# Attention in blocks of queries: the products with the values are issued one step later

## The chip, the cores and the metric

The kernel runs on one core of a Trainium2 chip. The metric is the device time of one execution in microseconds (us), as a median of repeated runs. The core has a matrix engine (PE, whose weight loader PEld loads the stationary operand of each matmul), a vector engine (DVE), a scalar engine (ACT), GpSimd (POOL), and the sync engine (SP), which issues most transfers. Each engine works through its own instructions in the order in which they stand; semaphores make one wait for another.

## The reference, cut to what matters

One layer of a decoder: a recurrent branch and an attention branch are merged, then comes a mixture of experts. The change touches the attention branch only: 8 heads, 1024 tokens, causal, in blocks of 128 queries.

```python
    for s0 in range(0, S, Q_BLOCK):                  # Q_BLOCK = 128, S = 1024
        e = s0 + Q_BLOCK
        s = jnp.einsum("bqhd,bkhd->bhqk", q[:, s0:e], k[:, :e]).astype(jnp.float32) * scale
        mask = jnp.arange(e)[None, :] <= (s0 + jnp.arange(Q_BLOCK))[:, None]
        p = jax.nn.softmax(jnp.where(mask, s, -jnp.inf), axis=-1).astype(v.dtype)
        outs.append(jnp.einsum("bhqk,bkhd->bqhd", p, v[:, :e]))
    o = jnp.concatenate(outs, axis=1).reshape(B, S, N_HEADS * V_DIM)
    return o @ w_mla_o
```

Query block `qb` has `(qb + 1) * 128` keys, so block 7 has 1024 and block 0 has 128.

## The kernel before, in words

The program is one long straight line of stages: the input projections and the recurrent branch; the products of the recurrent branch; the attention (from about 591 us to 893 us of the span); the product with `w_mla_o` and the merge (to about 987 us); the product with `w_out` with the routing (to about 1102 us); then the experts, two to a tile of 128 rows, whose weights stream in from HBM.

Products in nearly full precision are made of three matmuls each: every operand is split into a high part (rounded by ACT, `hi_of`, L113) and a low part (the rest, by a subtraction on DVE or POOL, `lo_of`, L116), and `mm3` (L118 to L121) adds high by high, high by low and low by high.

The attention works on 64 pairs (head, block of queries), in each head in the order 6, 7, 4, 5, 2, 3, 0, 1. Each pair goes through two functions, and each two blocks through a third:

- `attn_a` (L679): the scores on PE (L693; five matmuls for up to 512 keys, ten beyond), into one of two score buffers `s` in PSUM; on DVE the mask and the row's minimum (L697); on ACT the exponential (L702); on DVE the reciprocal of the sum and the scaling (L704, L705) to the probabilities `P`.
- `attn_b` (L708): PE transposes `P` in pieces of 128 (L720) into a PSUM bank `tp`, ACT writes the high part `pth` and DVE the low part `ptl`. Two blocks of queries fill one such pair of tiles side by side; there are two buffers of each (`PT = 2`).
- `attn_c` (L724): after the second block of a pair, the products with the values: three matmuls for each block of keys (L119 `pth` by `vh`, L120 `ptl` by `vh`, L121 `pth` by `vl`), 6, 12, 18 or 24 in all, into another bank `tp`; ACT copies it out (`ot`, L735) and SP sends it to DRAM (L736).

The loop at L826 issues, at step n, `attn_a` of pair n, `attn_b` of pair n - 2 (`LA = 2`), and `attn_c` if that pair was the second of two. Between the steps it issues background work of the next heads: the products for queries, keys and values of the next two heads (`tokens_block`, L582), their norms (`tokens_end`, L606; its chain of small operations on DVE is `rsqrt`, L92 to L108), the rotation on POOL (`head_chain`), and the transposes of queries and keys (`head_T`, L646: `ks`, `qs`, `kp`, `qp`, four matmuls each, evicted by ACT and then DVE). All of these, and `attn_b` and `attn_c`, share four PSUM banks named `tp`.

The order in which these functions are called is not the order in which the instructions stand. A scheduler of the framework places the instructions of each engine when the program is built, by the order of the calls as a priority and by its own estimates of when operands and buffers are free.

Of the kernel before, what the change touches and what calls it, by code (L numbers as in the profile page):

```python
# [51 lines left out]
def block_kernel(ctx, tc, x, positions, norm1_g, w_in, conv_w, conv_b, lru_wa, lru_ba, lru_wx,  # L52
# [65 lines left out]
    def mm3(ps, lh, ll, rh, rl, start, stop):  # L118
        nc.tensor.matmul(ps, lh, rh, start=start, stop=False)  # L119
        nc.tensor.matmul(ps, lh, rl, start=False, stop=False)  # L120
        nc.tensor.matmul(ps, ll, rh, start=False, stop=stop)  # L121
# [437 lines left out]
    with pool_of(name="hd", bufs=2) as hd, \  # L559
# [119 lines left out]
        def attn_a(h, qb):  # L679
            pr, j = pairs[h // 2], h % 2  # L680
            t, rr_ = pr["t", j], pr["rr"]
            e = (qb + 1) * 128
            qsl = slice(qb * 128, e)
            ps = sps.tile([128, S], F32, name="s")
            w = e if e <= 512 else e // 2
            nw = e // w
            psv = ps.rearrange("p (a b) -> p a b", b=512)[:, 0:nw, 0:w]
            for ch in range(nw):
                cc = slice(ch * w, ch * w + w)
                for n, (a, b, r) in enumerate((("qnh", "knh", 128), ("qnh", "knl", 128),  # L690
                                               ("qnl", "knh", 128), ("qpe", "kph", 128),
                                               ("qpe", "kpl", 128))):
                    nc.tensor.matmul(psv[:, ch], t[a][0:r, qsl], t[b][0:r, cc],  # L693
                                     start=n == 0, stop=n == 4)

            nm_ = tiny.tile([128, 1], F32, name="nm_")
            nc.vector.tensor_tensor_reduce(  # L697
                psv, psv, mask[:, S - e:S].rearrange("p (a b) -> p a b", b=w),
                rr_[:, qb, j:j + 1], 3.0e38, ALU.add, ALU.min, nm_)
            P = pp.tile([128, S], F32, name="P")  # L700
            sm = tiny.tile([128, 1], F32, name="sm")
            nc.scalar.activation(P[:, 0:e].rearrange("p (a b) -> p a b", b=w), psv, AF.Exp, bias=nm_, scale=-1.0,  # L702
                                 accum_out=sm)
            nc.vector.reciprocal(sm, sm)  # L704
            nc.vector.tensor_scalar(P[:, 0:e], P[:, 0:e], sm, None, op0=ALU.mult)  # L705
            Ps[h, qb] = P

        def attn_b(h, qb):  # L708
            P = Ps.pop((h, qb))
            o0 = (qb % 2) * 128  # L710
            for w in range(qb // 4 + 1):
                if (h, qb // 2, w) not in quads:
                    quads[h, qb // 2, w] = (pp.tile([128, 4, 256], F32R, name="pth", bufs=PT),
                                            pp.tile([128, 4, 256], F32R, name="ptl", bufs=PT))
                ph_, pl_ = quads[h, qb // 2, w]
                n = min(4, qb + 1 - 4 * w)
                pt = tps.tile([128, 4, 128], F32, name="tp")
                for kb in range(n):
                    k_ = (4 * w + kb) * 128
                    nc.tensor.transpose(pt[:, kb], P[:, k_:k_ + 128], ident)  # L720
                hi_of(ph_[:, 0:n, o0:o0 + 128], pt[:, 0:n])
                lo_of(pl_[:, 0:n, o0:o0 + 128], pt[:, 0:n], ph_[:, 0:n, o0:o0 + 128], nc.vector)

        def attn_c(h, g):  # L724
            pr, j = pairs[h // 2], h % 2
            vh, vl = pr["vh"][j], pr["vl"][j]
            po = mps.tile([128, 256], F32, name="tp")
            last = 2 * g + 1
            for kb in range(last + 1):
                o0 = 128 if kb == last else 0  # L730
                ph_, pl_ = quads[h, g, kb // 4]
                mm3(po[:, o0:256], vh[:, kb], vl[:, kb], ph_[:, kb % 4, o0:256],
                    pl_[:, kb % 4, o0:256], kb == 0, kb == last)
            ot = pp.tile([128, 256], F32, name="ot", bufs=2)
            nc.scalar.activation(ot, po, AF.Copy)  # L735
            nc.sync.dma_start(o_d[h, :, g * 256:g * 256 + 256], ot)  # L736
# [84 lines left out]
        LA = 2  # L821
        QO = [6,7,4,5,2,3,0,1]
        WT = [1]*8
        seq = [(h, qb) for h in range(H) for qb in QO]
        bg, total, done, mdone = [], 0.0, 0.0, 0.0
        for n in range(len(seq) + LA):  # L826
            if n < len(seq):
                h, qb = seq[n]
                if qb == QO[0]:
                    for c, f, a in bg:  # L830
                        f(*a)
                    bg = bg_work(h)
                    total = max(1e-9, sum(c for c, f, a in bg))
                    done = mdone = 0.0
                attn_a(h, qb)
                mdone += WT[QO.index(qb)] / sum(WT) * 1.05
            if n >= LA:
                h2, qb2 = seq[n - LA]
                attn_b(h2, qb2)
                if QO.index(qb2) % 2:  # L840
                    attn_c(h2, qb2 // 2)
            if n < len(seq):
                while bg and done / total <= mdone:
                    c, f, a = bg[0]
                    if f.__name__ == "tokens_start" and QO.index(qb) < LA:
                        break
                    bg.pop(0)
                    f(*a)
                    done += c
# [745 lines left out]
```

## Time and profile before

| | |
|---|---|
| median of 3 runs | 1661.24 us (1660.24 to 1663.36) |
| the profiled execution | 1662.71 us, its span 1660.9 us, mean granted clock 0.964 |
| PE busy over the span | 91% |
| attention | 591 to 893 us |
| merge and `w_out` | 893 to 1102 us |
| experts | 1102 us to the end |

How to read the rows: a row of busy time by stretch gives, for each engine, the microseconds in which it was busy and how many instructions it ran, then the granted clock of PE as a share of full speed, the busy share of the DMA engines and GB/s. A row of waits gives who waited, for what, the total in us, how many times, and the longest. A row of the timeline gives the start, the duration, the engine, the line, the operation with output and inputs, and in brackets how long the engine sat idle before it and what ended that. PE's matmuls overlap in the records, so the pace is read from one start to the next.

### The profile page before, as it was taken

How to read it: one execution, taken by the hardware profiler on the slowest of the kernel's cores; microseconds unless marked ns; L12 is line 12 of the kernel's file. 1: busy time of each engine (PE TensorE's matmuls, PEld its weight loads, DVE VectorE, ACT ScalarE, POOL GpSimd, SP SyncE). 2: the span in 40 equal slices, each digit the busy share in tenths (PEclk: the TensorE clock that was granted, in tenths of full speed). 3: DMA queues.
4: the chain of work that ended last, by engine and by line, in shares of the span. 5: the costliest groups of instructions: out<-in, count | busy, mean ns of one | idle time of the engine just before them, and what ended most of it. 6: DMA issues, size and time to landing. Idle time of an engine off the chain costs nothing. (4 is left out here: it accounts for less than half of the span.)

```text
span 1660.9 us, 22272 instructions
## 1 busy us (share of the span) xinstructions
PE 1508.6 (91%) x8484; PEld 1141.0 (69%) x8484; DVE 723.9 (44%) x1859; ACT 499.1 (30%) x1088; POOL 470.6 (28%) x467
## 2 busy tenths in 40 slices
PE   5999999899999999999898999978998887888876
PEld 5988887788888888888787877865554453444443
DVE  7745556420001677787874446773321221221211
ACT  5324554641111366666664112210000000000000
POOL 3134443322221335252621431122221111211111
PEclk9999999899999999999999999998998997999989
DMA  6212221262345210101215655369999999999994
GB/s 193 58 47 65 58 75 55 69 224 88 102 143 171 89 39 14 36 14 36 76 33 171 221 191 197 134 244 392 364 416 418 418 419 417 414 400 411 416 405 162
DMA packets 129664, 327.71 MB, mean 197 GB/s; under 512 B 17367, under 2 KB 82337, under 8 KB 105108
## 3 DMA queue, kind: packets, MB, share of 16 engines
q1 hardware_dynamic: 111684, 295.57, 47.6%
q0 software_dynamic: 14848, 21.46, 3.6%
q10 hardware_dynamic: 3024, 9.24, 1.4%
q8 instruction: 68, 1.11, 0.3%
q14 instruction: 40, 0.33, 0.1%
HBM read 307.74 MB, written 48.59 MB: 215 GB/s over the span
## 5 line engine op out<-in xcount | busy, mean ns | idle before, releaser
L1339 PE MATMUL ph<-w,x 128*64 128x256 f32 x1104 | 163.1, 405 | 26.3 <-DMA w<-in_exp_w_dram 24.0
L116 POOL TENSOR_TENSOR w_lo<-w_raw,w_hi 128x1024 fp32r<-128x1024 f32 x40 | 98.8, 2470 | 266.3 <-ACT w_hi L113 265.7
L259 PE MATMUL pp<-uTh,w_hi 128*128 128x512 f32 x496 | 156.2, 396 | 1.1 <-ACT xp L368 1.1
L262 PE MATMUL pp<-uTl,w_hi 128*128 128x512 f32 x496 | 155.9, 395 | 0.0
L265 PE MATMUL pp<-uTh,w_lo 128*128 128x512 f32 x496 | 155.7, 395 | 0.0
L1339 PEld LDWEIGHTS ph<-w,x 128*64 128x64 f32 x1104 | 94.7, 145 | 84.3 <-DMA w<-in_exp_w_dram 26.2
L1329 DVE SCALAR_TENSOR_TENSOR hs<-ph,rec_all,hs 128x256 f32<-128x256 f32 x32 | 15.4, 482 | 289.0 <-ACT hs L1328 289.0
L1356 ACT ACTIVATE hT<-pt 128x256 f32<-128x256 f32 x32 | 12.3, 384 | 343.0 <-PE pt L1354 343.0
L259 PEld LDWEIGHTS pp<-uTh,w_hi 128*128 128x128 f32 x496 | 93.5, 189 | 23.2 <-ACT xp L368 1.1
L262 PEld LDWEIGHTS pp<-uTl,w_hi 128*128 128x128 f32 x496 | 93.6, 189 | 22.3
L265 PEld LDWEIGHTS pp<-uTh,w_lo 128*128 128x128 f32 x496 | 93.3, 188 | 22.2
L1038 PE MATMUL px<-wo,ms 128*128 128x512 f32 x384 | 97.0, 401 | 1.0 <-DVE ms L116 1.0
L1339 PE MATMUL ph<-c,x 128*64 128x256 f32 x512 | 81.3, 413 | 13.0 <-DMA c<-in_exp_w_dram 12.9
L113 ACT ACTIVATE w_hi<-w_raw 128x1024 fp32r<-128x1024 f32 x40 | 42.1, 1053 | 139.2 <-PE pp L262 110.2
L1038 PEld LDWEIGHTS px<-wo,ms 128*128 128x128 f32 x384 | 70.2, 189 | 17.5 <-issue 1.8
L1339 PE MATMUL ph<-m,x 128*64 128x256 f32 x432 | 68.0, 414 | 14.0 <-DMA m<-in_exp_w_dram 10.9
L1339 PEld LDWEIGHTS ph<-c,x 128*64 128x64 f32 x512 | 47.5, 149 | 44.2 <-DMA c<-in_exp_w_dram 15.2
L116 DVE TENSOR_TENSOR cTl<-gt,cTh 128x1024 fp32r<-128x1024 f32 x4 | 4.9, 1225 | 164.5 <-ACT cTh L113 164.5
L1368 PE MATMUL py<-w,hT 128*64 128x512 f32 x288 | 71.1, 611 | 0.5 <-ACT hT L1356 0.5
L1339 PEld LDWEIGHTS ph<-m,x 128*64 128x64 f32 x432 | 39.0, 149 | 36.1 <-DMA m<-in_exp_w_dram 9.3
L897 PE MATMUL pp<-c,w 128*128 128x512 f32 x240 | 56.9, 392 | 0.0
L120 PE MATMUL tp<-ptl,vh 128*128 128x256 f32 (+1 forms) x160 | 47.8, 299 | 9.7 <-DVE ptl L116 9.3
(657 smaller groups left out, 3379.3 us busy)
## 6 DMA issues: line engine op xcount, KB each, us to landing
w<-in_exp_w_dram SPq DMA_DIRECT2D x101, 1024.0 KB, 22.4
c<-in_exp_w_dram SPq DMA_DIRECT2D x50, 1024.0 KB, 23.3
m<-in_exp_w_dram SPq DMA_DIRECT2D x40, 1024.0 KB, 22.4
w_raw<-in_w_in_dram SPq DMA_DIRECT2D x32, 512.0 KB, 5.0
xt<-in_x_dram SPq DMA_DIRECT2D x8, 512.0 KB, 5.3
hg_d<-hh SPq DMA_DIRECT2D x8, 512.0 KB, 2.6
gt<-hg_d SPq DMA_DIRECT2D x8, 512.0 KB
sgb_d<-gt SPq DMA_DIRECT2D x8, 512.0 KB, 5.2
```

What stands on the lines that cost most here:

```text
L113: nc.scalar.activation(dst, src, AF.Copy)
L116: eng.tensor_tensor(dst, src, f32v(hi), op=ALU.subtract)
L120: nc.tensor.matmul(ps, lh, rl, start=False, stop=False)
L259: nc.tensor.matmul(ps[:, s_], wh[:, k], ah[:, k, s_], start=k == 0, stop=False)
L262: nc.tensor.matmul(ps[:, s_], wh[:, k], al[:, k, s_], start=False, stop=False)
L265: nc.tensor.matmul(ps[:, s_], wl[:, k], ah[:, k, s_], start=False, stop=k == KD - 1)
L897: nc.tensor.matmul(pb[:, s_], w[:, a, k], oT[k][b][:, s_], start=k == 0 and a + b == 0, stop=k == KD - 1 and a == 1)
L1038: nc.tensor.matmul(px[:, s_], ms[:, a, k], wos[k][:, b, s_], start=k == 0 and a + b == 0, stop=k == KD - 1 and a == 1)
L1329: nc.vector.scalar_tensor_tensor(hs, ph[:, 256:512], rst, hs, op0=ALU.mult, op1=ALU.mult)
L1339: pe(nc.tensor.matmul(ph[64 * j:64 * j + 64, wi * 256:wi * 256 + 256], xT[:, k, 64 * j:64 * j + 64], w[2 * wi + j][:, k * 256:k * 256 + 25 ...
L1356: nc.scalar.activation(hT, pt, AF.Copy)
L1368: pe(nc.tensor.matmul(py[64 * j:64 * j + 64], hT[:, kk, 64 * j:64 * j + 64], w2[j][:, o_:o_ + 512], start=kk == 0, stop=kk == 1))
```

## The change

The call of `attn_c` is kept back by one step of the loop. When the second block of a pair has gone through `attn_b`, the pair is only noted in `pv`; in the next step `attn_a` of the next block is called first, then `attn_c` of the noted pair, then that step's `attn_b`. The loop runs one step longer for the last pair. The background work of a step now stands between `attn_b` and the `attn_c` that belongs to it. Nothing is added or removed: every function is called as often as before, with the same arguments.

```diff
         bg, total, done, mdone = [], 0.0, 0.0, 0.0
-        for n in range(len(seq) + LA):
+        pv = None
+        for n in range(len(seq) + LA + 1):
             if n < len(seq):
                 h, qb = seq[n]
                 ...
                 attn_a(h, qb)
                 mdone += WT[QO.index(qb)] / sum(WT) * 1.05
-            if n >= LA:
+            if pv:
+                attn_c(*pv)
+                pv = None
+            if LA <= n < len(seq) + LA:
                 h2, qb2 = seq[n - LA]
                 attn_b(h2, qb2)
                 if QO.index(qb2) % 2:
-                    attn_c(h2, qb2 // 2)
+                    pv = h2, qb2 // 2
```

What the scheduler makes of it stands in the order of the instructions. First place, PE in the second head: the transposes of block 5 (L720), the scores of block 0 (L693, 128 keys), the transposes of the next head's keys `kp` (L661), and the 18 products of blocks 4 and 5 (L119 to L121). Before:

```order
L720 MATMUL tp<-ident,P 128x128 x6
L693 MATMUL s<-knh,qnh 128x128
L693 MATMUL s<-knl,qnh 128x128
L119 MATMUL tp<-pth,vh 128x256
L661 MATMUL tp<-ident,kp 128x128 x4
L693 MATMUL s<-knh,qnl 128x128
L693 MATMUL s<-kph,qpe 128x128
L120 MATMUL tp<-ptl,vh 128x256
```

and with the change:

```order
L720 MATMUL tp<-ident,P 128x128 x6
L661 MATMUL tp<-ident,kp 128x128 x4
L693 MATMUL s<-knh,qnh 128x128
L693 MATMUL s<-knl,qnh 128x128
L693 MATMUL s<-knh,qnl 128x128
L693 MATMUL s<-kph,qpe 128x128
L693 MATMUL s<-kpl,qpe 128x128
L119 MATMUL tp<-pth,vh 128x256
L120 MATMUL tp<-ptl,vh 128x256
```

Before, the first product stood alone between two of the scores and the other seventeen came after the fourth score; now all eighteen stand together behind the fifth. A first product that stands alone occurs 29 times in the 32 groups of products before, and twice with the change, both in the last head.

Second place, ACT where the second head passes to the third: the copies of the next two heads' weights (`whq`, `whkv`, L113), the evictions of a product (`ot`) and of transposes (`pth`, `knh`, `qnh`), and the exponential of the third head's first block (L702, 896 keys). Before:

```order
L113 ACTIVATE whq<-P 128x768
L735 ACTIVATE ot<-tp 128x256
L666 ACTIVATE knh<-tp,pch 128x512
L113 ACTIVATE whkv<-P 128x1024
L702 ACTIVATE P,sm<-s,nm__5610 128x896
L666 ACTIVATE qnh<-tp,pch 128x512
```

and with the change:

```order
L113 ACTIVATE whq<-P 128x768
L735 ACTIVATE ot<-tp 128x256
L113 ACTIVATE pth<-tp 128x128
L666 ACTIVATE knh<-tp,pch 128x512
L702 ACTIVATE P,sm<-s,nm__5594 128x896
L666 ACTIVATE qnh<-tp,pch 128x512
L113 ACTIVATE kph<-tp 128x512
L113 ACTIVATE whkv<-P 128x1024
```

The exponential now stands ahead of the copy of `whkv` instead of behind it.

Third place, PE a little later in the same passage: the transposes of block 1 (L720), the scores of block 4 (L693, 320 keys in each half), the transposes of the head after (L661 `ks`), and the six products of blocks 0 and 1. Before:

```order
L720 MATMUL tp<-ident,P 128x128 x2
L693 MATMUL s<-knh,qnh 128x320
L693 MATMUL s<-knl,qnh 128x320
L693 MATMUL s<-knh,qnl 128x320
L693 MATMUL s<-kph,qpe 128x320
L119 MATMUL tp<-pth,vh 128x256
L693 MATMUL s<-kpl,qpe 128x320
```

and with the change:

```order
L720 MATMUL tp<-ident,P 128x128 x2
L661 MATMUL tp<-ident,ks 128x128 x4
L693 MATMUL s<-knh,qnh 128x320
L661 MATMUL tp<-ident,qs 128x128 x4
L693 MATMUL s<-knl,qnh 128x320
```

Two sets of transposes now stand ahead of these scores, and the products follow after all ten of them. From the product with `w_mla_o` on, the order on every engine is the same but for a few neighbouring rows near its start.

## The prediction

> **What bounds the kernel now.** I read the page's busy time first, then busy time by stretch, then the waits of the attention, then single passages of the timeline.
>
> ```profile
> PE 1508.6 (91%) x8484; PEld 1141.0 (69%) x8484; DVE 723.9 (44%) x1859; ACT 499.1 (30%) x1088; POOL 470.6 (28%) x467
> ```
>
> ```profile
> 591.00:893.00 302.00, 277.59 (x1761) 247.28 (x1762) 236.21 (x598) 191.30 (x567) 120.32 (x179) 0.98 0.11 36
> 893.00:987.00 94.00, 89.73 (x387) 73.12 (x387) 32.47 (x38) 19.54 (x20) 38.31 (x28) 0.98 0.64 210
> 987.00:1102.00 115.00, 111.72 (x593) 91.42 (x592) 78.32 (x444) 26.92 (x71) 17.94 (x19) 1.00 0.47 170
> 1102.00:1650.00 548.00, 466.30 (x3128) 260.01 (x3127) 130.04 (x277) 32.23 (x75) 107.40 (x106) 0.93 0.98 396
> ```
>
> PE is the bound until 1102 us, the transfers behind it (0.98 of the DMA engines). The attention is the first stretch: 302.00 us, PE busy for 277.59, so PE stands still for 24.4 us, and DVE is busy for 236.21. The next two stretches hang on PE (89.73 of 94.00, 111.72 of 115.00), and the experts follow them, so whatever the attention gains or loses should shift everything behind it one to one.
>
> Who makes PE wait in the attention, PE's own rows:
>
> ```profile
> PE tp L120 <- DVE ptl L116: 9.3, 9, 4.7
> PE tp L119 <- ACT pth L113: 3.8, 11, 0.7
> PE tp L119 <- DVE qnl L667: 3.7, 2, 1.8
> ...
> PE tp L119 <- DVE rs_y L108: 1.4, 1, 1.4
> PE tp L661 <- DVE sm L704: 0.5, 1, 0.5
> PE tp L661 <- DVE kpl L116: 0.3, 1, 0.3
> ```
>
> and the largest of its weight loader, which goes ahead of PE and so counts waits that PE partly fills:
>
> ```profile
> PEld tp L119 <- ACT pth L113: 13.9, 27, 2.1
> ```
>
> Most of it stands before the products with the values: a group's first product waits for the high part of the transposed probabilities (L119 for `pth`), its second for the low part (L120 for `ptl`).
>
> **The change part by part.** No engine gets more or less work; only places change, and less than the diff says: the scheduler had already put most of the next block's scores between a group's first product and the rest. New is that a group stays together behind all of them.
>
> A. *The lone first product.* Blocks 4 and 5 of the second head, PE:
>
> ```profile
> 664.39 0.30 PE L693 MATMUL s<-knh,qnh 128*128 128x128 f32 x1
> 664.53 0.27 PE L693 MATMUL s<-knl,qnh 128*128 128x128 f32 x1
> 665.10 0.39 PE L119 MATMUL tp<-pth,vh 128*128 128x256 f32 x1 [0.29 <-ACT pth L113]
> 665.32 0.60 PE L661 MATMUL tp<-ident,kp 128*128 128x128 f32 x4
> ...
> 666.10 0.28 PE L121 MATMUL tp<-pth,vl 128*128 128x256 f32 x1
> 666.22 0.28 PE L119 MATMUL tp<-pth,vh 128*128 128x256 f32 x1
> ```
>
> These scores follow each other by 0.14 us, so the product was due at 664.67 and began at 665.10, with other work ready behind it. Inside the group the step is 0.12 us; from the lone product to what follows it is 0.22, some 0.10 lost each time. Of the 29 lone products 27 go: 2.7 us of such steps, and PE's own wait for `pth`, 3.8 us. Where `ptl` is then waited for, in 9 groups, part is given back: I take 2.0 us. A: 4.5 us. Bounds: nothing, if `ptl` always comes last; 13.9 + 2.7 = 16.6, if all of the loader's wait were lost.
>
> B. *Two long waits of a first product* (3.7 us), where one pair of heads passes to the next. The product needs a `tp` bank which the transposed queries free when DVE has taken `qnl` from it. PE, DVE and ACT in one of the two passages:
>
> ```profile
> 672.05 0.28 PE L120 MATMUL tp<-ptl,vh 128*128 128x256 f32 x1
> ...
> 673.29 0.41 PE L693 MATMUL s<-knh,qnl 128*128 128x448 f32 x1
> ...
> 681.12 0.48 PE L119 MATMUL tp<-pth,vh 128*128 128x256 f32 x1 [1.85 <-DVE qnl L667]
> ```
>
> ```profile
> 674.14 1.16 DVE L697 CUSTOM_DVE_ANT_0 s<-s,mask,rr__4901 128x896 f32<-128x896 f32 x1 [1.81 <-PE s L693]
> ...
> 680.24 0.74 DVE L667 SCALAR_TENSOR_TENSOR qnl<-tp,pch,qnh 128x512 fp32r<-128x512 f32 x1
> ```
>
> ```profile
> 674.57 0.69 ACT L666 ACTIVATE knh<-tp,pch 128x512 fp32r<-128x512 f32 x1
> 676.33 1.06 ACT L113 ACTIVATE whkv<-P 128x1024 fp32r<-128x1024 f32 x1 [1.06 <-DMA P<-in_w_ukv_dram]
> 677.29 0.99 ACT L702 ACTIVATE P<-s,nm__5610 128x896 f32<-128x896 f32 x1
> ```
>
> The mask of block 6 waits until its scores are done at 674.14, since eleven products (672.05 to 673.29, 1.24 us) cut into them; with the lone one that is 1.35 us. Then ACT copies `whkv`, which waits for a transfer, before the exponential; on DVE the scaling of this block stands ahead of `qnl`. With the change the products stand behind the scores and the exponential ahead of `whkv`: it can start when `knh` ends at 675.26 instead of at 677.29, 2.0 us sooner, and `qnl` follows. But transposes that need the same bank now stand ahead of block 4's scores, four of which PE did before its stop (about 4 x 0.15 = 0.6 us), so that work is still to do. Gain 1.4 each, 2.8 for both. Bounds 0 and 3.7.
>
> The clock goes with it, as busy time by stretch shows (last numbers: granted clock, DMA share, GB/s):
>
> ```profile
> 677.00:681.00 4.00, 2.23 (x11) 1.46 (x10) 2.50 (x4) 3.20 (x7) 2.37 (x1) 1.00 0.00 0
> 681.00:685.00 4.00, 3.88 (x19) 3.84 (x19) 3.69 (x6) 1.27 (x2) 0.00 (x0) 0.57 0.02 4
> ...
> 757.00:761.00 4.00, 2.23 (x13) 1.67 (x11) 2.58 (x4) 3.12 (x7) 2.39 (x1) 1.00 0.00 0
> 761.00:765.00 4.00, 3.12 (x23) 2.83 (x24) 3.92 (x7) 2.57 (x5) 0.00 (x0) 1.00 0.00 0
> ...
> 808.00:813.00 5.00, 0.54 (x4) 0.28 (x3) 4.93 (x10) 0.04 (x1) 2.54 (x2) 0.79 0.72 204
> ```
>
> After the first stop PE ran at 0.57 for 4 us, which costs 4 x 0.43 = 1.7 us; after its twin at 757 it did not. With half the stop left I count half of it, 0.9 us (0 to 1.7). [...]
>
> C. *The waits for `ptl`*, 9.3 us. The longest, 4.7, is the last row above: DVE busy for 4.93 of 5.00 us. Small operations of the norms of the next heads stretch there, such as
>
> ```profile
> 805.96 2.30 DVE L106 TENSOR_TENSOR rs_t<-rs_t,rs_v 128x16 f32<-128x16 f32 x1
> ```
>
> for 16 columns, while POOL runs its splits. Products that come later don't help a DVE that is full, so nothing of it. Of the other 4.6 us I take 1.0: the six products of blocks 0 and 1 now have all of block 4's scores ahead of them, three more than before, 0.15 us each, in eight heads, and in part of these they waited. Bounds 0 and 4.6.
>
> D. *One wait of 1.4 us* (`rs_y`), of the products for the next heads' queries on a bank, in the first head. Their order changes there; I take half, 0.7 (0 to 1.4).
>
> E. *What becomes late next.* The transposes of the next head (L661) are now more often ahead of the scores. Where their bank is not free yet, all of PE stands behind them, and the block's mask and exponential behind PE. Today they make PE wait for 0.5 + 0.3 us in all. Outside B I take a loss of 1.0; bounds 0 and, if half of 56 sets (7 heads, 2 halves, 4 kinds) waited for one eviction of 0.74 us (`qnl` above), 21 us. The later copy of a product (`ot`) and its transfer to DRAM have no reader in these stages but the loads for the product with `w_mla_o`, and at the end of the last head the order is as before, so SP's queue costs nothing here.
>
> Sum: 4.5 + 2.8 + 0.9 + 1.0 + 0.7 - 1.0 = 8.9 us. The profiled execution would go from 1662.71 us (its span 1660.9) to 1653.8; it lies 1.5 above the median of the runs, so the median goes from 1661.24 to 1652.3 us.
>
> **The rivals.** *No change.* DVE, not the order on PE, sets the pace. For it: where PE stood longest DVE was full, and the scheduler had already done most of this move. Then A is given back at `ptl` in every group and only B's shorter stops, 2.8 less E's 1.0, remain: 1659.4 us. Against it: DVE is busy for 236.21 of 302.00 us, so on average it has 66 us to spare, and 27 of the loader's waits are for `pth`, which ACT makes.
>
> *Slower.* The transposes of the next head block the scores (E). Every one that stands ahead of scores and finds no free bank costs PE an eviction on DVE, 0.74 us. Without E the gains are 9.9 us, so from 9.9 / 0.74, some 13 such waits, the change loses; at 22 they cost 16.3 us, and the time is 1661.24 - 9.9 + 16.3 = 1667.6 us. For it: the four banks are shared by everything, and in B one such bank is what PE waits for. Against it: the two rows for L661 above come to 0.8 us, and with the change a group holds its own bank for a shorter time, since its products stand together.
>
> *Much faster.* If all of PE's 24.4 us but the stop of 4.7 and D's half went, 24.4 - 4.7 - 0.7 = 19.0, the time would be 1642.2. Against it: some waits stand at the end of the last head, where the order is the same.
>
> *The change does not do what it says.* On PE most of the products were behind the scores before; this is the first rival with its mechanism, and I give it no chance of its own.
>
> **How the numbers follow.** A difference under 0.2%, 3.3 us, is about what a measurement of this kernel cannot tell from none. Chances: the forecast, a gain of 3.3 to 15 us, 0.62; no change 0.21; slower 0.13; much faster 0.04. So faster 0.66, within 0.2% 0.21, slower 0.13. The likeliest is 1652.3 us. Its own range, with A and B at half and at one and a half times what I took, is 1648.6 to 1656. For eight in ten I reach up past the first rival to 1663, and down to 1644 for A's upper bound: 1644 to 1663. Left out are most of the slower case and half of the much faster one.
>
> **What would show it.** In the changed kernel's profile: PE's idle time in the attention falls from 24.4 to about 15 us; the loader's row for L119 on `pth` falls from 27 waits to under 10 (A); the two waits on `qnl` shrink to under half, or turn up as short waits of L661 (B); the waits on `ptl` stay near 9 us with one long one (C); the attention ends some 9 us sooner and the stretches behind it keep their lengths. I am wrong in A if the row for `ptl` grows by what the row for `pth` loses; in E if L661 turns up with more than some 5 us of waits; and in the carry to the end if the attention becomes shorter and the expert stage longer.

## The result, and the profile after

| | before | after | ratio (95% interval) |
|---|---|---|---|
| median, first comparison | 1660.93 us | 1645.16 us | 0.9902 (0.9887 to 0.9917) |
| the same kernel again | 1659.39 us | 1646.65 us | 0.9924 (0.9894 to 0.9953) |
| a third time | 1659.24 us | 1646.70 us | 0.9916 (0.9899 to 0.9933) |

The change makes the kernel faster by 15.8, 12.7 and 12.5 us in the three comparisons. 1645.16 us lies inside the range, 1.2 us from its lower end; the gain is larger than the 8.9 us of the forecast. The profiled executions went from 1662.71 to 1644.16 us, by 18.55 us. Three single executions of kernels further down took 2164, 2422 and 4354 us and count in none of the ratios.

Busy time by stretch of the changed kernel, with the columns of the rows of before (length; PE, PEld, DVE, ACT, POOL with their instructions; granted clock; DMA share; GB/s):

```profile
588.80:877.60 288.80, 268.24 (x1764) 243.92 (x1765) 235.38 (x598) 190.75 (x567) 120.38 (x179) 0.99 0.12 38
877.60:971.00 93.40, 89.81 (x390) 72.58 (x389) 34.85 (x40) 20.30 (x21) 39.21 (x30) 1.00 0.65 217
...
1086.00:1634.00 548.00, 456.19 (x3092) 250.75 (x3090) 128.12 (x270) 31.13 (x73) 108.59 (x107) 0.95 0.98 395
```

The attention is some 13 us shorter, and PE is idle in it for 288.80 - 268.24 = 20.6 us, against 24.4 before. The larger part of the gain, 277.59 - 268.24 = 9.35 us, stands in PE's busy time, though the matmuls are the same: a matmul behind a wait or at a lower clock had a longer record (for 128x256 before, 0.28 us inside a group, 0.38 behind the wait of 0.50 us at 628.07, and 0.41 at a granted clock of 0.50 from 631.37 on). For the reckoning below I therefore take the distance from each matmul's start to the next.

PE's waits in the attention, and the two rows of its weight loader that matter:

```profile
PE tp L120 <- DVE ptl L116: 10.5, 9, 5.9
PE tp L661 <- DVE qnl L667: 1.8, 2, 0.9
PE tp L720 <- DVE sm L704: 1.4, 1, 1.4
PE tp L661 <- ACT ot L735: 1.4, 1, 1.4
PE tp L661 <- DVE ptl L116: 1.2, 2, 0.6
PE tp L119 <- ACT pth L113: 1.2, 2, 0.7
PE tp L720 <- DVE ptl L116: 1.0, 2, 0.5
PE s L693 <- ACT P L702: 0.9, 1, 0.9
```

```profile
PEld tp L120 <- DVE ptl L116: 13.5, 12, 6.1
...
PEld tp L119 <- ACT pth L113: 1.7, 2, 0.9
```

The loader's row for `pth` fell from 13.9 us in 27 waits to 1.7 in 2. The waits on `qnl` halved and stand at L661 now. The row for `ptl` did not shrink, it grew.

From first scores to first scores of the next head, the heads last, in us (worked out from the trace; the last column is the whole attention up to the first product with `w_mla_o`):

| kernel | 1 | 2 | 3 | 4 | 5 | 6 | 7 | 8 | all |
|---|---|---|---|---|---|---|---|---|---|
| before | 50.3 | 28.4 | 51.2 | 28.7 | 50.2 | 35.9 | 28.5 | 28.9 | 302.2 |
| after | 45.9 | 29.3 | 46.7 | 29.3 | 46.8 | 34.5 | 27.8 | 28.4 | 288.8 |
| after, again | 45.9 | 29.3 | 46.7 | 29.4 | 46.7 | 34.3 | 27.8 | 28.4 | 288.5 |
| after, third | 45.9 | 29.3 | 46.6 | 29.3 | 46.8 | 35.3 | 27.8 | 28.4 | 289.5 |
| first alone | 47.3 | 29.7 | 47.9 | 29.3 | 47.9 | 36.8 | 27.5 | 28.3 | 294.7 |
| inner groups | 45.9 | 29.9 | 46.9 | 29.9 | 46.9 | 36.2 | 28.9 | 29.2 | 293.8 |
| groups at passages | 48.8 | 27.6 | 50.5 | 28.1 | 48.0 | 35.8 | 27.7 | 28.6 | 295.1 |
| first head only | 45.9 | 29.5 | 49.8 | 28.7 | 49.8 | 35.9 | 28.5 | 28.9 | 297.0 |
| `whkv` first | 46.0 | 29.3 | 47.0 | 29.3 | 47.0 | 35.1 | 27.8 | 28.4 | 289.7 |
| low part first | 38.5 | 40.0 | 49.8 | 30.3 | 50.9 | 36.0 | 30.0 | 30.1 | 305.7 |
| two splits on DVE | 45.9 | 29.3 | 46.8 | 29.3 | 46.8 | 35.9 | 27.8 | 28.4 | 290.3 |
| splits late | 46.0 | 29.3 | 46.7 | 29.3 | 46.6 | 29.3 | 34.9 | 28.4 | 290.5 |
| splits spread | 45.9 | 29.3 | 46.8 | 29.3 | 46.7 | 29.3 | 27.6 | 29.2 | 284.2 |

The three profiles of the changed kernel agree head by head within 0.2 us, but for the sixth head. The time up to the attention, which no kernel here changes, varies from 588 to 595 us between profiles, so the attention's length tells more than one execution's time. Heads 1, 3 and 5, in which PE also makes the next heads' queries, keys and values, give nearly all of the gain. In the run "low part first", 61 matmuls of the first head stand in the second, so these two compare only as a sum.

Where the attention's time beyond the undisturbed pace went, by what the trace names as the releaser (each matmul's distance to the next one, less the median distance behind its line and shape in the kernel before, 257.6 us in sum for both; the parts are good to some 0.3 us):

| PE late for | before | after |
|---|---|---|
| `pth` | 5.6 | 1.5 |
| `ptl` | 10.7 | 15.1 |
| `qnl` | 4.0 | 2.15 |
| `rs_y` (a bank) | 1.6 | 0 |
| the exponential (`P`) | 2.8 | 1.05 |
| `sm`, `kpl`, `qpe` | 3.7 | 1.6 |
| `ot` (a bank) | 0.4 | 1.6 |
| nothing named: switches and slow clock | 15.8 | 8.2 |
| sum | 44.6 | 31.2 |

### The profile page after: what moved, and what is told of

Read it like the earlier page. It is cut to its first block, busy times and chain, and to the rows that moved or that the text cites. A ratio compares the mean times of both kernels' runs of the same rounds, so it can differ in the third digit from the quotient of the medians.

```text
span 1642.4 us, 22281 instructions
## 1 busy us (share of the span) xinstructions
PE 1488.4 (91%) x8484; PEld 1127.5 (69%) x8484; DVE 724.9 (44%) x1859; ACT 498.5 (30%) x1088; POOL 469.5 (29%) x467
## 5 line engine op out<-in xcount | busy, mean ns | idle before, releaser
L1343 PE MATMUL ph<-w,x 128*64 128x256 f32 x1104 | 157.4, 396 | 26.7 <-DMA w<-in_exp_w_dram 25.2
L1343 PEld LDWEIGHTS ph<-w,x 128*64 128x64 f32 x1104 | 90.0, 142 | 86.0 <-DMA w<-in_exp_w_dram 27.1
L113 ACT ACTIVATE w_hi<-w_raw 128x1024 fp32r<-128x1024 f32 x40 | 42.1, 1053 | 138.7 <-PE pp L262 112.6
L1343 PE MATMUL ph<-m,x 128*64 128x256 f32 x432 | 64.3, 392 | 15.1 <-DMA m<-in_exp_w_dram 12.0
L1343 PEld LDWEIGHTS ph<-c,x 128*64 128x64 f32 x512 | 44.9, 144 | 46.6 <-DMA c<-in_exp_w_dram 19.8
L1343 PEld LDWEIGHTS ph<-m,x 128*64 128x64 f32 x432 | 37.2, 140 | 35.3 <-DMA m<-in_exp_w_dram 10.5
L116 DVE TENSOR_TENSOR ptl<-tp,pth 128x512 fp32r<-128x512 f32 (+2 forms) x96 | 50.7, 551 | 19.9 <-ACT pth L113 19.6
L120 PE MATMUL tp<-ptl,vh 128*128 128x256 f32 (+1 forms) x160 | 46.8, 292 | 10.8 <-DVE ptl L116 10.5
```

The costliest lines, as they stand in the source:

```text
L113: nc.scalar.activation(dst, src, AF.Copy)
L116: eng.tensor_tensor(dst, src, f32v(hi), op=ALU.subtract)
L1343: pe(nc.tensor.matmul(ph[64 * j:64 * j + 64, wi * 256:wi * 256 + 256], xT[:, k, 64 * j:64 * j + 64], w[2 * wi + j][:, k * 256:k * 256 + 25 ...
```

## The experiments

All kernels compute the same layer; only orders change, and in one of them the engine of two splits.

**The lone product put back.** The change, with each group's first product issued behind its transposes again:

```diff
+        def attn_c0(h, g):          # the first product: vh[0] by pth[0], into po
+            ...
                 if QO.index(qb2) % 2:
                     pv = h2, qb2 // 2
+                    attn_c0(*pv)
```

> The change, but each group's first product (high by high part of the first key block) is issued right behind its transposes again; the other 5 to 23 products stay where the change put them. Theory T1 (the gain is that a group stays together: the lone product waits for pth, holds up the scores behind it, and each switch to and from it costs about 0.1 us): most of the gain is lost, attention 288.8 -> 296 to 300 us, time 1652 to 1657 us, 27 or more waits of the loader for pth again. Theory T2 (the gain comes from the passages between head pairs, where the exponential goes ahead of whkv, and from the order in the first heads): attention 289 to 292 us, time 1645 to 1648 us. A result between says how the gain splits.

Measured: 1653.25 us against 1658.03 before, ratio 0.9966 (0.9955 to 0.9977); attention 294.7 us. PE's waits and the loader's, L729 being the lone product:

```profile
PE tp L729 <- ACT pth L113: 6.6, 14, 1.0
...
PE tp L119 <- DVE rs_y L108: 0.4, 1, 0.4
```

```profile
PEld tp L729 <- ACT pth L113: 12.2, 25, 1.4
```

Undoing the lone product alone takes 5.2 to 6.2 us of the attention's gain back, with 25 of the 27 waits of the loader. Of the 7.5 us that stay, some 2.5 belong to two slow spells of the clock in the profile of before (worked out under "The first head only" and in the last part), so of the 10.9 us that are left for the order somewhat more than half hangs on the lone product. The medians agree: 4.8 us of gain are left, beside 12.5 to 15.8. By its time the result is T1's, by its attention it lies between the two theories.

**Only the inner groups, and only those at the passages.** Two complements, each with half the groups one step later:

```diff
                 if QO.index(qb2) % 2:
-                    pv = h2, qb2 // 2
+                    if qb2 in (7, 5):          # in the other kernel: (3, 1)
+                        pv = h2, qb2 // 2
+                    else:
+                        attn_c(h2, qb2 // 2)
```

> Products come one step later only for the groups of blocks 6,7 and 4,5; those of 2,3 and 0,1 are issued at once as before. T1: half of the lone products (16 of 32) are gone and with them about half of what keeping together brings (5 us), plus what the first heads' order brings: attention 294 to 296 us, 1651 to 1654 us. T2: the passages keep their 2 us stops, since the groups of 0,1 stand as before: attention 298 to 301 us, 1655 to 1659 us.

> The counterpart: one step later only for the groups of blocks 2,3 and 0,1, which stand at the passages from head to head. T1: about half of what keeping together brings (4 to 5 us) and the two passages (3 us): attention 294 to 296 us, 1651 to 1654 us. T2: most of the gain: attention 289 to 292 us, 1645 to 1649 us.

Measured: inner groups 1652.23 us, 0.9951 (0.9935 to 0.9967), attention 293.8; groups at the passages 1653.75 us, 0.9972 (0.9962 to 0.9983), attention 295.1. The two gains in the attention, 8.4 and 7.1 us, add up to 15.5, some 2 more than both at once; but the slow spells of before are in both. Without them (2.5 us, and an estimated 1 us for the one spell of the second kernel in these heads) the gains are 5.9 and 5.6 beside 10.9. That is T1's split by size, but the place is a surprise: with the inner groups alone the stops on `qnl` are gone from PE's waits, although the eleven products at the passages still stand among the first block's scores. (That kernel waits more for `P` instead, 10.8 us in 4 waits; the longest, 6.7, stands in the sixth head, where the others wait for `ptl`.) With the other half they remain:

```profile
PE tp L661 <- DVE qnl L667: 3.0, 2, 1.9
```

ACT in that kernel's first passage:

```profile
672.37 0.69 ACT L666 ACTIVATE knh<-tp,pch 128x512 fp32r<-128x512 f32 x1
673.97 1.06 ACT L113 ACTIVATE whkv<-P 128x1024 fp32r<-128x1024 f32 x1 [0.91 <-DMA P<-in_w_ukv_dram]
674.93 0.99 ACT L702 ACTIVATE P<-s,nm__5594 128x896 f32<-128x896 f32 x1
...
675.91 0.68 ACT L666 ACTIVATE qnh<-tp,pch 128x512 fp32r<-128x512 f32 x1
```

`whkv`, which waits for a transfer, stands ahead of the exponential and of `qnh`, as in the kernel before. In its second passage it does not, and the stop there is 1.1 us instead of 1.9.

**`whkv` ahead of the exponential.** To test that reading, the change with the first block's exponential ordered behind the copy:

```diff
+            if qb == QO[0] and j == 0 and 0 < h < 6:
+                # order on ACT: the exponential behind the copy of whkv
+                tc.add_manual_dep(ex.ins, pairs[h // 2 + 1]["cp"].ins.name, ...)
```

> The change, but at the two passages from head pair to head pair the exponential of the first block is ordered behind ACT's copy of whkv again, as it was before; products and scores stay where the change put them. Theory T3 (the 1.8 us stops at the passages come from the copy standing ahead of the exponential: the run that delays only the inner groups lost the stops with the products of the passages left as before, and the run that delays only those at the passages kept them): the stops on qnl return, from 0.9 to about 1.9 us each, the clock may fall behind one of them: attention 288.8 -> 291 to 294 us, ratio 0.991 to 0.994. Rival T2' (the prediction's other half: the eleven products that cut into the first block's scores set the stop): no stop returns, attention 288.5 to 289.5 us, ratio as the changed kernel's.

Measured: 1648.79 us against 1659.39, ratio 0.9928 (0.9907 to 0.9949), beside 0.9924 of the changed kernel in the same comparison; attention 289.7 us. PE's waits and ACT in the first passage:

```profile
PE s L693 <- ACT P L702: 2.1, 3, 0.9
...
PE tp L661 <- DVE qnl L667: 0.3, 2, 0.2
```

```profile
671.62 0.70 ACT L666 ACTIVATE qnh<-tp,pch 128x512 fp32r<-128x512 f32 x1
...
674.40 1.06 ACT L505 ACTIVATE whkv<-P 128x1024 fp32r<-128x1024 f32 x1 [1.11 <-DMA P<-in_w_ukv_dram]
675.37 0.99 ACT L702 ACTIVATE P<-s,nm__5594 128x896 f32<-128x896 f32 x1
```

The stops on `qnl` did not come back; two waits of the scores for `P` came in their place, and each of the two heads is 0.2 to 0.3 us longer. T3 falls as it was put. What the profiles agree on is another order: the stop is long, 1.4 to 1.9 us, in the five passages where the copy stands ahead of `qnh` (both of before and of the first head only, the first of groups at the passages), and at most 1.1 us where `qnh` goes first (after, inner groups, first alone, this one, and the second passage of groups at the passages). That is read off seven kernels; no run changed this order by itself, and the run here also put `qnh` ahead of the exponential.

**The first head only.** The kernel before, with the products one step later only for the first head:

```diff
                 if QO.index(qb2) % 2:
-                    attn_c(h2, qb2 // 2)
+                    if h2 == 0:
+                        pv = h2, qb2 // 2
+                    else:
+                        attn_c(h2, qb2 // 2)
```

> The kernel before, with the products one step later only in the first head (the first 8 blocks of queries). Theory T4 (step D is mis-sized: in the first head the order alone is worth 4.4 us, since the products for the next heads' queries no longer wait for rs_y behind a lone product): first head 50.3 -> 45.9 us, later heads as before, attention about 298 us, ratio 0.997. Rival T1 (only keeping together counts, four groups a head): first head 49.5 to 49.9 us, attention 301.4 to 301.8 us, ratio 0.9995.

Measured: 1657.52 us against 1659.39, ratio 0.9989 (0.9978 to 0.9999); first head 45.9 us, exactly as with the whole change, second head 29.5. T4 holds in the profile: 4.4 us in one head, 1.1 given back in the next. But the time moved by 1.9 us only. Most of the rest was the clock of one execution. Before, the stop on `rs_y` in the first head was followed by a slow spell; in the kernel with the groups at the passages the same stop was not, and its first head took 48.8 us instead of 50.3. Both by stretch:

```profile
630.00:634.00 4.00, 4.00 (x20) 4.00 (x20) 2.20 (x13) 0.45 (x4) 1.73 (x3) 0.57 0.00 0
```

```profile
630.00:634.00 4.00, 4.00 (x27) 3.85 (x28) 2.90 (x14) 1.03 (x6) 1.58 (x2) 1.00 0.00 0
```

20 matmuls at a clock of 0.57 against 27 at 1.00. PE's order in the two kernels is the same up to this stop and for 69 matmuls behind it, and those took 13.30 and 11.77 us: the spell cost 1.5 us. Without it the first head gains 2.9, less the 1.1 given back 1.8: what the medians show.

**Together, but not later.** The kernel before, called as before; each block of keys takes its product with `ptl` first, so that a group can only start when it can also go on:

```diff
-                mm3(po[:, o0:256], vh[:, kb], vl[:, kb], ph_[:, kb % 4, o0:256],
-                    pl_[:, kb % 4, o0:256], kb == 0, kb == last)
+                for x_, y_, f_ in ((vh, pl_, 0), (vh, ph_, 1), (vl, ph_, 2)):
+                    nc.tensor.matmul(po[:, o0:256], x_[:, kb], y_[:, kb % 4, o0:256], ...)
```

> The kernel before, not delayed, but each block of keys takes the product with the low part (ptl) first, so that a group's first product needs what its second needed and all 32 groups stand together; the scheduler places them. Theory T1 (keeping a group together is worth 4 to 6 us, in whatever step it is called, part of it because no lone product holds one of the four tp banks while it waits): the waits on pth (3.8 us) and on rs_y (1.4 us) go, the attention falls from 302.2 to 294 to 298 us, time ratio 0.995 to 0.997. Rival T7 (together only pays if the group also comes later): PE waits for ptl instead, by as much as for pth before; attention 300.5 us or more, ratio 0.999 to 1.001.

Measured: 1664.89 us against 1658.88, ratio 1.0035 (1.0020 to 1.0051): slower. Attention 305.7 us. Its PE (L733 are the products):

```profile
PE tp L733 <- DVE ptl L116: 27.8, 22, 5.7
```

```profile
704.94 0.27 PE L693 MATMUL s<-kpl,qpe 128*128 128x128 f32 x1
706.19 0.39 PE L733 MATMUL tp<-ptl,vh 128*128 128x256 f32 x1 [0.97 <-DVE ptl L116]
706.41 0.28 PE L733 MATMUL tp<-pth,vh 128*128 128x256 f32 x1
```

No lone product is left, no wait on `pth` or `rs_y`, and PE waits for `ptl` 22 times instead. T1 as I had put it is wrong: a whole group is not worth 4 to 6 us wherever it stands. T7 has the direction, but the loss is larger than it said (300.5 us or more, 0.999 to 1.001). The run does more than keep groups together, though. Between a group's last transposes and its first product with `ptl` the scheduler placed 7.9 other matmuls here (mean of the first 30 groups), 10.5 in the kernel before and 12.5 with the change: the groups came not only no later, but sooner. No run keeps a group whole at the place where its other products stood, so how much of the loss is due to that, and whether the lone product was useful filler before, stays open.

**The stop in the sixth head.** It grew from 4.7 to 5.9 us. DVE and POOL of the changed kernel there:

```profile
793.23 2.32 DVE L105 TENSOR_TENSOR rs_t<-rs_y 128x16 f32<-128x16 f32 x1
795.58 2.26 DVE L106 TENSOR_TENSOR rs_t<-rs_t,rs_v 128x16 f32<-128x16 f32 x1
```

```profile
793.12 2.40 POOL L116 TENSOR_TENSOR w<-c,w 128x1024 fp32r<-128x1024 f32 x1
795.48 2.34 POOL L116 TENSOR_TENSOR c<-c,c 128x1024 fp32r<-128x1024 f32 x1
```

Each small operation begins 0.1 us behind a split and ends with it. Three kernels moved the splits. First two of them to DVE:

```diff
-        w2s[i] = split(..., raw, nc.gpsimd)
+        w2s[i] = split(..., raw, nc.gpsimd if i else nc.vector)
...
-            oT[h] = split(t, raws[h], nc.gpsimd)
+            oT[h] = split(t, raws[h], nc.gpsimd if h else nc.vector)
```

> The change, and the first two of the splits that the background work of the later heads gives to POOL go to DVE. In the changed kernel two 16-column operations of the next heads' norms take 2.3 us each on DVE beside two of POOL's splits of 2.4 us, and PE then stands for 6.0 us. If the two engines hinder each other (T1's reading of the 4.7 us wait that the change left alone), the small operations take 0.2 us, DVE pays some 0.6 to 1 us for each split it now makes, and PE's stop falls from 6.0 to 2.5 to 4 us: 1641 to 1643 us. If DVE is simply full there, the stop stays near 6 us: 1645 to 1647 us.

Measured: 1648.32 us, 0.9936 (0.9919 to 0.9952), attention 290.3: slower than both forecasts. The two small operations took 0.16 and 0.18 us, but the wait moved (lines stand one further down in this kernel):

```profile
PE tp L120 <- DVE ptl L116: 6.2, 8, 2.1
PE tp L662 <- POOL ks L626: 3.9, 1, 3.9
```

The longest wait on `ptl` is 2.1 us, but PE then stands 3.9 us for the rotated keys: no gain. Next, all six splits behind the rotations of the last head pair:

```diff
-        BG = ((("l", 0), ("L", 0, 0), ("s", 1), ("L", 0, 1), ("S", 1, 0)),
-              (("L", 0, 2), ("S", 0, 1), ...
+        BG = ((("l", 0), ("L", 0, 0)),
+              (("s", 1), ("L", 0, 1), ("S", 1, 0), ("L", 0, 2), ("S", 0, 1), ...
+        # and on POOL, every split is ordered behind the last rotation
```

> The change, and POOL makes its splits of w_mla_o and of the outputs of heads 0 to 4 (six subtractions of 128x1024) only behind the rotations of the last head pair, in heads 6 and 7; their loads move with them. Theory T5 (the 6 us stop in the sixth head comes from the two splits that run beside the two 16-column operations of the norms): both take 0.2 us again instead of 2.3, the stop shrinks to 1 to 2.5 us, the sixth head goes from 34.5 to 30 to 31.5 us: attention 284.5 to 286 us, ratio 0.987. Rival T6 (DVE and the rotations on POOL are full there anyway, as the run with two splits on DVE suggests, where the stop turned up as a wait for ks instead): the sixth head stays at 33.5 us or more, attention 288 us or more; if the splits come late for the product with w_mla_o, that stretch grows from 91.6 us by up to 3 us.

Measured: 1647.64 us, 0.9927 (0.9907 to 0.9947), attention 290.5. The sixth head fell to 29.3 us, as T5 says, and the seventh rose to 34.9. There ACT stood at the head of its queue for a load, with the transposed probabilities behind it:

```profile
826.51 1.06 ACT L113 ACTIVATE c<-c 128x1024 fp32r<-128x1024 f32 x1 [3.54 <-DMA c<-o_d]
827.48 0.36 ACT L113 ACTIVATE pth<-tp 128x256 fp32r<-128x256 f32 x1
```

So the loads and splits were dealt out anew over the last two heads, and ACT's copies ordered one by one behind exponentials there (in part):

```diff
+        hi = nc.scalar.activation(t[:, 0], raw, AF.Copy)
+        # order on ACT: head 1 behind the exponential of (6, 5), head 2 behind (6, 2),
+        # head 3 behind (7, 6), head 4 behind (7, 5)   (head, block; heads from 0)
```

> The change, with POOL's six splits behind the rotations of the last head pair as in the run with late splits, and ACT's copies for them ordered behind exponentials one after the other over heads 6 and 7, since ACT stood 3.5 us for a load in the sixth-but-one head there with the transposed probabilities queued behind it. If that wait made the 7.1 us that the late splits gave back: heads 6 and 7 (counted from one) 29.3 and 29 to 31 us, last head 28.4 to 29.5 us, attention 284 to 286.5 us, ratio 0.987 to 0.990. If POOL's splits hinder DVE wherever they stand: attention 288 us or more, ratio as the changed kernel's 0.990 to 0.993.

> The changed kernel again, on the same chip and in the same rounds as the next run: ratio 0.989 to 0.993, attention 288 to 289.5 us, no granted clock under 0.9 in the first five heads (no stop there is longer than 1.6 us apart from the one at the start of the first head).

> The kernel with the splits spread over the last two heads again, beside the changed kernel: if the 4.6 us that its attention was shorter in one profile reach the end, its ratio is 0.002 to 0.004 under the changed kernel's (attention 283.5 to 285 us); if the experts' transfers or the merge take it back, the two ratios agree within 0.001.

Measured: 1643.12 us, 0.9907 (0.9885 to 0.9929), and 1643.21 us, 0.9897 (0.9880 to 0.9914), attention 284.2 us both times. The unaltered change in the second comparison: 1646.70 us, 0.9916 (0.9899 to 0.9933). Its waits and its attention:

```profile
PE tp L120 <- DVE ptl L116: 6.6, 9, 0.9
```

```profile
588.00:872.30 284.30, 266.88 (x1764) 242.30 (x1764) 229.89 (x599) 190.81 (x567) 121.51 (x179) 1.00 0.12 39
```

The attention is 4.3 to 5.3 us shorter, and at 1.00 the clock did not fall in it. Side by side its ratio is 0.0019 under the changed kernel's, at the edge of what was expected, and the intervals of the two overlap; over all runs, 9 of this kernel have a mean of 1643.0 us and 13 of the unaltered change 1646.4, so 3.5 us less, give or take about 2 (95%, from their spreads of 2.0 and 2.5). It is the fastest kernel here. The same two operations in it, with POOL's splits elsewhere:

```profile
792.57 0.18 DVE L105 TENSOR_TENSOR rs_t<-rs_y 128x16 f32<-128x16 f32 x1
792.78 0.17 DVE L106 TENSOR_TENSOR rs_t<-rs_t,rs_v 128x16 f32<-128x16 f32 x1
```

0.18 and 0.17 us instead of 2.32 and 2.26. In the kernel before, L106 took 2.30 us at 805.96 beside a split of POOL (805.86, 2.38 us), and 0.17 at 811.28, with POOL idle from 810.53 to 813.79. What makes these operations long beside a split is not shown.

## Why the prediction was right, and where it was not

**Direction and range** held. The size was short: 8.9 us against 12.5 to 15.8 in the medians, the last just above the 3.3 to 15 us that the forecast was given, and 18.2 between the two profiles up to the product with `w_out` (18.55 at the end). The range reached down to 1644 us for A's upper bound, which A never came near; what took the time there were terms priced at nothing, the clock and `x`. That it held is in part luck; its own range of 1648.6 to 1656 was missed on the fast side. Term by term, in the profiles:

- **A and C** (4.5 and 1.0). By the table the waits on `pth` and what has no name brought 4.1 + 7.6 = 11.7, of which some 2.5 are the clock, so about 5 are left for switches; `ptl` took back 4.4. Net 4.8, against 5.5. (What has no name also holds waits of under 0.15 us.) The run with the lone product put back says 5.9. (In the traces 31 groups have their first product parted from the rest before and 3 with the change, one of them in the seventh head, so 28 lone products went, not 27.) C had the wrong sign: nothing of the short waits for `ptl` went, and the long one grew. The warning that the `ptl` row would grow came true: with the rows of L661 and L720, PE's waits for `ptl` rose by 3.4 us, and those for `pth` fell by 2.6. So by this reckoning A's gain came through its steps between kinds of work, which it had at 2.7, and not through the waits. A's reason was half right. It priced the lone product as a loss in itself, wherever the rest of the group stands; "the lone product put back" bears that out behind the change, and "together, but not later" shows that a whole group called too soon for `ptl` loses more than it saves.
- **B** (2.8): 1.85. The waits did turn up at L661. The step that fails is the cause: neither the eleven products nor the exponential's place set the stop by itself, since it went in one kernel that kept the products there (inner groups) and in one that put the exponential back (`whkv` first).
- **The clock** (0.9): 2.5. I counted half of one slow spell, at 1.7 us. The profile of before held two in the first five heads; one stands in the first head, which I had not looked at. It cost 1.5 us. The one in the third head cost 1.0: the 79 matmuls from that stop on stand in the same order in the kernel with the first head only and took 14.12 us before, 13.15 there. With the change the stops at the passages are 0.9 us, and in three profiles none of them was followed by a slow spell.
- **D** (0.7): 1.6, the whole wait.
- **E** (-1.0): -1.2 for the bank of `ot`; the waits of L661 for `ptl` stand in C.
- **No term.** The waits of scores for `P` and of others for `sm`, `kpl` and `qpe` lost 1.75 and 2.1 us. I had priced none of them; each is a single wait or a few.
- **The carry.** "The stretches behind keep their lengths" failed at one place. PE's wait for `x` in the product with `w_mla_o`, before and after:

```profile
PE pp L897 <- ACT x L113: 4.3, 1, 4.3
```

```profile
PE pp L901 <- ACT x L113: 2.7, 1, 2.7
```

That stretch fell from 94.2 to 91.6 us. In the ten profiles whose last group of the last head comes later it took 91.5 to 92.8 us, in the four others 94.2 to 94.9. So it belongs to the change; which transfer or copy makes it was not settled. The experts kept theirs (533.6 and 532.9 us).

The differences: clock 1.6, no term 3.85, D 0.9, `x` 2.6, the time before the attention 2.2 (which varies by itself), less B 0.95, A and C 0.7, E 0.2: 9.3 us, and 8.9 + 9.3 = 18.2. Without the clock's 2.5 and the 2.2 ahead of the attention, 13.5 are left, not far from the 12.5 and 12.7 of the later comparisons.

**The rivals.** "No change" said that A would be given back at `ptl`: 4.4 us of it was. "Slower" needed 13 waits for a bank: the rows of L661 above hold five, with 4.4 us. Idle PE of about 15 us was wrong as a sign (20.6), since most of the gain lies in busy time.

## What to carry to other kernels

When products wait for a chain on other engines, put the whole group one step later. Each half of this alone brought less or lost: the later place for all but the first product gained 4.8 us, whole groups that come no later, and want `ptl` sooner, cost 6 us. Count the gain from start to start of PE's instructions, not from its idle time, and price the many waits of a few tenths as well as the few long ones. Compare one stretch over several profiles before a term is read from one execution: slow spells of the clock behind short stops come and go (here behind 4 of 57 stops of 1.2 to 2.5 us).

## What was not expected of the hardware

The clock. In the 14 profiles all 11 stops of PE of over 4 us in the attention were followed by a slow spell, at a granted clock of 0.50; of the 57 between 1.2 and 2.5 us (from start to start) only 4 were, and the same stop had one in one kernel and none in another. (A fifth stood inside a spell that a stop of 2.65 us had begun.) One of the four came behind a wait of 1.35 us in the first head before, in a stretch of 4 us in which PE was busy for 2.15:

```profile
626.00:630.00 4.00, 2.15 (x16) 1.77 (x15) 3.41 (x14) 3.00 (x16) 2.60 (x5) 1.00 0.00 0
```

The traces also tell which stops had one. In every profile the changes of the granted clock lie whole multiples of 3.41 us apart. Split at these points, the attentions of the 14 profiles give 1160 stretches at a granted clock of 1.00: all 16 in which PE's records cover 46% or less were followed by one at 0.50, and none of the 1144 with 49% or more. The first head's stop before (followed by a slow spell), the twin stop at 757 that kept its clock, and the first head's stop with the groups at the passages, which kept it too:

```profile
626.59:630.01 3.42, 1.57 (x11) 1.19 (x10) 3.38 (x14) 2.42 (x12) 2.01 (x4) 1.00 0.00 0
759.71:763.12 3.41, 2.06 (x15) 1.87 (x15) 3.35 (x5) 1.19 (x4) 0.06 (x1) 1.00 0.00 0
```

```profile
628.48:631.89 3.41, 2.06 (x15) 1.97 (x15) 3.38 (x19) 1.15 (x6) 0.40 (x1) 1.00 0.00 0
```

So in these rows what looked like chance goes with where a stop falls on this grid: the first lies inside one stretch, of which PE was busy for 46% (1.57 of 3.42 us); the twin reaches over the point at 759.71, and PE was busy for 60% (2.06 of 3.41) behind it and for 86% (2.93 of 3.41) ahead; the third left PE 60%. The grid lay differently against the kernel in each profile: counted in steps of 3.41 us, one of its points stands at 630.01 us before and at 630.68 with the change. The same split shows the way back: a stretch at 0.50 was followed by one at 1.00 in all 16 cases with PE busy for 89% or more, and by another at 0.50 in all 13 with 84% or less.
